# Entry of the odd layer: ctx's sums behind the fourth tile, two query projections inside the chain, mask and sinks on ScalarE

## The chip, the cores and the metric

The kernel runs on one core of a Trainium2 chip. The metric is device microseconds of one launch; lower is better. TensorE (PE) multiplies matrices, VectorE (DVE), ScalarE (ACT) and GpSimd (POOL) do elementwise work, and SyncE (SP) issues transfers. The engines run on their own and meet at semaphores; each works its own queue in order.

## The reference

A transformer of two layers over 512 rows of x and 256 rows of a context (ctx), width 1024. Layer 0 (even) mixes with a gated MLP and differential attention, layer 1 (odd) with banded attention over x's keys plus all keys of ctx; each layer is followed by a gated FFN. What matters here is the odd layer's entry:

```
a  = rmsnorm(h,  norm1_g) * (1 + sc1)  + sh1        # 512 rows
ac = rmsnorm(hc, norm1_g) * (1 + csc1) + csh1       # 256 rows of ctx
q, k, v = split(a @ w_qkv)      # 1024, 256, 256 columns
kc, vc  = split(ac @ w_qkv[:, 1024:])
q, k = rope(q), rope(k)
# block of 128 queries: keys of 3 blocks (masked to |distance| <= 128) and all of ctx, plus a sink
p = softmax([q k^T / 8 + mask, q kc^T / 8, sink])
o = p[keys] @ v + p[ctx] @ vc
```

There are 16 query heads and 4 key heads of 64 columns.

## The kernel before

Rows lie along the free axis and columns of the model along the 128 partitions, eight tiles (k = 0 to 7) to the width of 1024. A product in near-fp32 precision is three matmuls (`mm3`, L110 to 117): high weights by high data, high by low, low by high. Weights arrive by DMA as fp32 ("raw"), ScalarE casts the high half and GpSimd subtracts to make the low half.

`seam` runs from the end of the FFN of layer 0 to the keys and values of layer 1. Most of its instructions go through `run`, which chains them: each stands on its engine behind the one written before. What isn't chained (rotations, stacks, copies) is placed by the scheduler of the framework, by written order as priority and by simulated times; `issue_after` puts an instruction behind a given one, and `high_priority` gives a block an earlier place in the written order.

The order in `seam`:
- last FFN products, residuals, and squares of h for the norm. `sums` multiplies the squares by a matrix of ones; `diagonal` makes the inverse root from the sums in nine small VectorE steps and a tenth that puts it on a diagonal ("q"); `spread` multiplies that by ones and so lays it over all partitions.
- x's norm gives rx. Then, by the string of steps at L1471, for each tile k: modulation of x ("t", and its low half "l"), residuals of ctx ("c"), weights ("w"), and the products named by `order` (L1455): "K3" is tile 3 of the keys, "V3" of the values, "s" ctx's sums, "d" ctx's spread. Before the change "s" stands behind K6 and sums two tiles, since GpSimd has added the squares of tiles 1 to 6 to tile 0.
- query projection 0 (`qps`, in the PSUM bank "fill"), then for each tile ctx's modulation and its products with the key and value weights (`k_c`, `v_c`).
- the rotation of the keys (`rope`: shuffle and a product on VectorE, a product and an add on GpSimd), their high and low stacks (`stack`), mask, identity and sinks, copies of the values.

`odd` rotates and stacks query projection 0, computes projections 1 to 7 (L1556; one bank "fill" for all but projection 1) and, per group g of four heads, attends: scores in a wide PSUM tile (L1584, L1592, mask L1589), maximum, exponential, transposes (L1621), products with the values (L1632). PSUM has eight banks: three "b", one "f", and either four singles or two wide tiles.

Of the kernel before, what the change touches and what calls it, by code (L numbers as in the profile page):

```python
# [27 lines left out]
class Builder:  # L28
# [235 lines left out]
        nc.gpsimd.tensor_tensor(sh, sh, tabs[1], ALU.mult)  # L264
        nc.gpsimd.tensor_tensor(out, out, sh, ALU.add)

    def stack_q(self, q, pool, T, tag, bufs, s=1.0, eng=None):
        nc = self.nc
        qa = pool.tile([P, T], F32R, name=self.uid("qa"), tag=tag, bufs=bufs)
        qb = pool.tile([P, T], F32R, name=self.uid("qb"), tag=tag, bufs=bufs)  # L270
        A, B = slice(0, 64), slice(64, 128)
        nc.scalar.mul(qa[A], q[A], s)
        nc.scalar.mul(qb[B], q[B], s)
        for lo, hi, X, Y in ((qa, qa, A, B), (qb, qb, B, A)):
            if s == 1.0:
                (eng or nc.vector).tensor_tensor(lo[Y], q[X], hi[X].bitcast(F32), ALU.subtract)
            else:
                nc.vector.scalar_tensor_tensor(lo[Y], q[X], s, hi[X].bitcast(F32), ALU.mult, ALU.subtract)
        return qa, qb
# [1032 lines left out]
    def seam(self, s2_part, Wl, ahead):  # L1312
# [32 lines left out]

        def square(who, m):
            T = (TX, TC)[who]
            sq[who, m] = Qp.tile([P, T], F32, name=self.uid("sq"), tag=f"sq{who}", bufs=8)
            run("ACT", nc.scalar.activation, sq[who, m], self.h(who, m), AF.Square)

        def add(key, who, to, m):
            run(key, {"DVE": nc.vector, "POOL": nc.gpsimd}[key].tensor_tensor, sq[who, to], sq[who, to], sq[who, m], ALU.add)

        def sums(ps, tiles, T):
            n = T // P
            for i, t in enumerate(tiles):
# [50 lines left out]
        sums(ps, [sq[0, m] for m in (0, 3, 7)], TX)  # L1407
        for m in (0, 1):
            c_residual(m)
        c_unit(2, self.bank)  # L1410
        for m in (3, 4):
            c_unit(m, self.single)
# [39 lines left out]
                run("PE", self.mm3, acc[4 + tb], [t[:, tb * P:(tb + 1) * P] for t in C[k]], v_w(k), k == tb == 0,  # L1452
                    k == KT - 1)

        order = iter("K0 V0 K1 V1 K2 V2 K3 V3 K4 V4 K5 V5 K6 s K7 V6 d V7".split())  # L1455
        csum = []

        def products(upto):
            for v in order:
                if v == "s":  # L1460
                    csum.append(self.single())
                    sums(csum[0], [sq[1, 0], sq[1, 7]], TC)
                elif v == "d":
# [6 lines left out]
        rests = {}  # L1470
# [21 lines left out]
        for k in range(KT):  # L1492
            t, c = Wq[k // 4], k % 4 * P
            run("PE", self.mm3, qps, (t[:, 0, c:c + P], t[:, 1, c:c + P]), X[k], k == 0, k == KT - 1)
        kc = self.single()
        kc = [kc[:, n * TC:(n + 1) * TC] for n in range(2)]
        b = self.bank()
# [8 lines left out]
        kfs = [Rt.tile([P, TA], F32, name=self.uid("kf"), tag="kf", bufs=2) for _ in range(2)]  # L1506
        K = []
        for n in range(2):
            self.rope(kps[n], kfs[n][:, :TX], tabs)
# [10 lines left out]

        for n in range(2):
            stack(n, slice(0, TX))
        for n in range(2):
            nc.scalar.copy(kfs[n][:, TX:], kc[n])
            stack(n, slice(TX, TA))
        mask = Rk.tile([P, 2, P], F32R, name="mask")
        identr = Rk.tile([P, P], F32R, name="identr")
        sink = Rk.tile([P, 16], F32, name="sink2")
        with tc.issue_after(self.tail["DVE"].ins):
            nc.vector.tensor_copy(mask, mraw.rearrange("p (a c) -> p a c", a=3)[:, 0::2, :])  # L1530
            nc.vector.tensor_copy(identr, self.ident)
            nc.vector.tensor_copy(sink, nsink)
            nc.vector.tensor_scalar(nsink, nsink, -1.0, None, ALU.mult)
        with tc.issue_after(self.tail["ACT"].ins):
            nc.scalar.activation(self.small(16), nsink, AF.Exp)
        V = []
        for tb in range(6):
            v = Rk.tile([P, TC], F32, name=f"v1_{tb}")
# [3 lines left out]
        self.close_ring()  # L1542
        self.ring, self.ring_cfg = kept
        Rt.release()
        self.kv = qps, X, Rk, tabs, K[0] + K[1], V, mask, identr, sink, nsink

    def odd(self):
        tc, nc, a = self.tc, self.nc, self.a
        self.wp.release()
        self.open_wide()  # L1550
        qps, X, Rk, tabs, K, V, mask, identr, sink, nsink = self.kv
        Rs = tc.alloc_tile_pool(name="att1", bufs=1, side="right", reuse_waits="tile")
        Qs = {}

        def project_q(n):
            ps = (self.bank if n == 1 else self.fill)() if n else qps  # L1556
            if n:
                with tc.issue_after(self.tail["ACT"].ins) if n < 3 else ExitStack():
                    W = self.blocks(a["q1"][n])
                self.dense(ps, W, X)  # L1560
            qf = Rs.tile([P, TX], F32, name=self.uid("qf"), tag="qf", bufs=2)
            self.rope(ps, qf, tabs)
            Qs[n] = self.stack_q(qf, Rs, TX, "sq", 16, 0.125)

        def softmax(g, i, rc):

# [39 lines left out]
        def part():  # L1606
            return Rs.tile([P, 512], F32, name=self.uid("pt"), tag="pt", bufs=6)
# [173 lines left out]
```

## Time and profile before

| | us |
|---|---|
| median of three runs | 1585.23 |
| lowest and highest | 1578.97, 1585.93 |
| profiled execution | 1583.56 |
| its span | 1581.5 |
| granted clock, mean over the span | 0.988 |

The span is what the profiler saw between the first and the last instruction; the execution's own time is 2.06 us more. The stage that is edited lies between about 905 and 1010 us of the span; attention runs until about 1190. In rows of the timeline the first number is the start and the second the length; matmuls are pipelined, so a matmul's cost is the distance to the next start. "x24" merges 24 records of one kind; a matmul on fp32 data that aren't split leaves two records. In brackets stands the idle time of the engine before the row, and who ended it.

### The profile page before, as it was taken

The numbers are of one execution on the slowest core, as the hardware profiler recorded it, in microseconds if no ns is written. First come the engines' busy times: TensorE is split into PE (matmuls) and PEld (weight loads), VectorE is DVE, ScalarE is ACT, GpSimd is POOL, SyncE is SP. The second block draws the span as 40 slices with busy tenths as digits, with TensorE's granted clock in tenths as the row PEclk, the third lists the DMA queues.
The fourth block names the chain that finished last, engine by engine and source line by source line (L and its number), as shares of the span: only waits on it lengthen the run. The fifth ranks groups of instructions, "written<-read, shape, count | busy, mean of one in ns | idle before, by whom it ended". The sixth has DMA issues, their size and how long they took to land.

```text
span 1581.5 us, 24959 instructions
## 1 busy us (share of the span) xinstructions
PE 1520.5 (96%) x9547; PEld 1355.7 (86%) x9547; DVE 1082.6 (68%) x1942; ACT 728.7 (46%) x1486; POOL 831.6 (53%) x562
## 2 busy tenths in 40 slices
PE   6999988999999999999999998999999999999998
PEld 4776877889989999999999987777869989999997
DVE  4720788765697787888786478665667976666665
ACT  2412676553553333333333345555655644444444
POOL 0463211060356776777776454531304399898982
PEclk9999999999999999999999999999999999999999
DMA  9845100033123333444552211100225233333301
GB/s 329 309 143 190 40 8 1 1 133 134 67 75 119 114 110 118 140 160 141 166 167 67 74 58 42 61 28 4 72 81 198 68 96 106 97 107 105 100 21 54
DMA packets 53415, 162.26 MB, mean 103 GB/s; under 512 B 6192, under 2 KB 8624, under 8 KB 45616
## 3 DMA queue, kind: packets, MB, share of 16 engines
q1 hardware_dynamic: 46240, 135.37, 25.6%
q10 hardware_dynamic: 7056, 25.30, 4.9%
q8 instruction: 75, 1.23, 0.3%
q14 instruction: 44, 0.36, 0.1%
HBM read 158.55 MB, written 2.10 MB: 102 GB/s over the span
## 4 chain that ended last, share of the span: by engine, by line
PE 85%; DVE 10%; ACT 3%; issue 1%; POOL 0%; DMA 0%; DVEq 0%; SPq 0%; ACTq 0%; POOLq 0%
PE pw L114 11%; PE pw L115 11%; PE pw L116 11%; PE pb L115 9%; PE pb L114 8%; PE pb L116 8%; PE pf L114 4%; PE pf L115 4%; PE pf L116 4%; PE pb L1632 2%; PE pb L1621 2%; PE pf L370 2%; PE pw L1584 1%; PE pw L1592 1%; PE pw L553 1%
## 5 line engine op out<-in xcount | busy, mean ns | idle before, releaser
L114 PE MATMUL pw<-ax,w 128*128 128x384 f32 (+2 forms) x732 | 233.9, 321 | 2.5 <-DVE q L49 1.9
L115 PE MATMUL pw<-ax,w 128*128 128x384 f32 (+2 forms) x732 | 233.8, 320 | 1.4 <-DVE ax L477 1.4
L116 PE MATMUL pw<-ax,w 128*128 128x384 f32 (+2 forms) x732 | 233.2, 319 | 0.1
L785 DVE SCALAR_TENSOR_TENSOR xT<-pb,mod,xT 128x512 f32<-128x512 f32 (+3 forms) x206 | 144.1, 706 | 128.8 <-PE pb L116 128.5
L91 POOL TENSOR_TENSOR w<-raw,w 128x512 fp32r<-128x512 f32 (+1 forms) x74 | 112.8, 1531 | 204.3 <-ACT w L88 182.0
L49 POOL TENSOR_TENSOR w<-raw,w 128x512 fp32r<-128x512 f32 x120 | 182.4, 1537 | 47.1 <-ACT w L49 47.0
L49 POOL TENSOR_TENSOR w<-t,w 128x512 fp32r<-128x512 f32 x99 | 148.1, 1499 | 56.0 <-ACT w L49 56.0
L114 PE MATMUL pb<-hh,w 128*128 128x512 f32 x480 | 171.4, 357 | 2.3 <-DVE xT L785 2.3
L116 PE MATMUL pb<-hh,w 128*128 128x512 f32 x480 | 171.8, 358 | 0.3 <-DVE w L49 0.3
L115 PE MATMUL pb<-hh,w 128*128 128x512 f32 x480 | 171.5, 357 | 0.0
L115 PE MATMUL pw<-T,w 128*128 128x384 f32 (+1 forms) x508 | 157.0, 310 | 1.2 <-DVE T L131 1.2
L114 PE MATMUL pw<-T,w 128*128 128x384 f32 (+1 forms) x508 | 156.3, 310 | 1.1 <-DVE hs L49 1.1
L116 PE MATMUL pw<-T,w 128*128 128x384 f32 (+1 forms) x508 | 157.0, 310 | 0.0
L114 PEld LDWEIGHTS pw<-ax,w 128*128 128x128 f32 x732 | 139.0, 190 | 9.5 <-DVE q L49 2.6
L115 PEld LDWEIGHTS pw<-ax,w 128*128 128x128 f32 x732 | 139.3, 190 | 7.7 <-DVE ax L477 3.1
L116 PEld LDWEIGHTS pw<-ax,w 128*128 128x128 f32 x732 | 139.5, 191 | 3.0 <-DVE w L954 0.4
L114 PE MATMUL pf<-ax,w 128*128 128x256 f32 (+2 forms) x412 | 136.9, 332 | 3.9 <-ACT f L596 2.8
L115 PE MATMUL pf<-ax,w 128*128 128x256 f32 (+2 forms) x412 | 136.1, 330 | 0.8 <-POOL ax L131 0.8
L116 PE MATMUL pf<-ax,w 128*128 128x256 f32 (+2 forms) x412 | 135.6, 329 | 0.0
L49 POOL TENSOR_TENSOR hh<-hs,hh 128x768 fp32r<-128x768 f32 (+1 forms) x42 | 80.8, 1925 | 90.0 <-ACT hh L49 67.6
L49 POOL TENSOR_TENSOR w<-rawo,w 128x512 fp32r<-128x512 f32 x59 | 104.1, 1764 | 29.8 <-ACT w L49 29.8
L239 DVE SCALAR_TENSOR_TENSOR junk<-ar,cb 128x1024 bf16<-128x1024 f32 x64 | 105.7, 1652 | 0.0
(403 smaller groups left out, 3961.4 us busy)
## 6 DMA issues: line engine op xcount, KB each, us to landing
raw<-ffn_in SPq DMA_DIRECT2D x44, 1024.0 KB, 5.2
ar<-ada SPq DMA_DIRECT2D x24, 1024.0 KB, 7.2
ar<-ada ACTq DMA_DIRECT2D x48, 512.0 KB, 3.5
rawo<-ffn_out SPq DMA_DIRECT2D x88, 256.0 KB, 3.0
raw<-odd_out SPq DMA_DIRECT2D x32, 256.0 KB, 2.7
raw<-qk SPq DMA_DIRECT2D x16, 256.0 KB, 7.6
raw<-uv SPq DMA_DIRECT2D x16, 256.0 KB, 2.7
raw<-even_out SPq DMA_DIRECT2D x8, 512.0 KB, 3.5
```

The source lines that it names most:

```text
L49: self.tail[key] = fn(*args, **kw)
L91: eng.tensor_tensor(lo, raw, hi.bitcast(F32), ALU.subtract)
L114: mm(out, s[0], m[0], start=start, stop=False, **kw)
L115: mm(out, s[0], m[1], start=False, stop=False, **kw)
L116: return mm(out, s[1], m[0], start=False, stop=stop, **kw)
L239: return self.nc.vector.scalar_tensor_tensor(junk, t, 1.0, self.cb[who], ALU.mult, ALU.mult, accum_out=self.acc[who][:, col:col + 1])
L370: nc.tensor.matmul(ps[32 * q:32 * q + 32, :w], cst[:, k, :], t[:, w * q:w * q + w], start=k == 0, stop=k == KT - 1, skip_group_check=True)
L553: nc.tensor.matmul(ps[:, :TX], Q[c][:, qs], K[c][p][:, :TX], start=p == 0, stop=p == 1)
L785: ins = self.nc.vector.scalar_tensor_tensor(h, ps[:, r], self.modcol(l, j, m, who), h, ALU.mult, ALU.add)
L1584: nc.tensor.matmul(ps[:, st:en], Q, K[g][p][:, b0 * P:b1 * P], start=p == 0, stop=p == 1, skip_group_check=True)
L1621: last = nc.tensor.transpose(pt[:, x * P:(x + 1) * P], es[2 * (x % 2) + x // 2][:, kb * P:(kb + 1) * P], self.ident)
L1632: nc.tensor.matmul(po[64 * h:64 * h + 64, :], V[vb][:, 64 * g:64 * g + 64], t[:, h * TC:h * TC + TC], start=kb == 0, stop=kb == nb - 1, sk ...
```

## The change

Four things in `seam`, two in `odd`:
- `order` has "s" behind V4 and sums six tiles; VectorE adds the square of tile 1 to tile 0, GpSimd that of tile 2. K7 stands behind V6. Squares of x that are only added to others share two buffers.
- the weights of query projection 1 are loaded and split in the chain as well (at "l7"), and the projection itself follows projection 0, in a single bank.
- mask, identity, sinks, their negation and the first exponential are chained on ScalarE behind the weights, where they stood on VectorE behind ctx's modulation.
- the keys' rotation is written before the query projections; each half of the keys is stacked for x and ctx before the other half.
- `odd` rotates and stacks queries 0 and 1 at the priority of the place behind the first half of the keys, into tiles in the pool of the keys; the wide PSUM pool opens behind them.
- the loop over groups projects queries from 2 on.

```diff
-    def stack_q(self, q, pool, T, tag, bufs, s=1.0, eng=None):
+    def stack_q(self, q, pool, T, tag, bufs, s=1.0, eng=None, out=None):
-        qa = pool.tile([P, T], F32R, name=self.uid("qa"), tag=tag, bufs=bufs)
-        qb = pool.tile([P, T], F32R, name=self.uid("qb"), tag=tag, bufs=bufs)
+        qa, qb = out or [pool.tile([P, T], F32R, name=self.uid(v), tag=tag, bufs=bufs) for v in ("qa", "qb")]
...
-            sq[who, m] = Qp.tile([P, T], F32, name=self.uid("sq"), tag=f"sq{who}", bufs=8)
+            tag, n = ("sqc", 8) if who else ("sqx", 3) if m in (0, 3, 7) else ("sqt", 2)
+            sq[who, m] = Qp.tile([P, T], F32, name=self.uid("sq"), tag=tag, bufs=n)
...
         for m in (0, 1):
             c_residual(m)
+        add("DVE", 1, 0, 1)
...
-        order = iter("K0 V0 K1 V1 K2 V2 K3 V3 K4 V4 K5 V5 K6 s K7 V6 d V7".split())
+        order = iter("K0 V0 K1 V1 K2 V2 K3 V3 K4 V4 s K5 V5 K6 V6 K7 d V7".split())
...
-                    sums(csum[0], [sq[1, 0], sq[1, 7]], TC)
+                    sums(csum[0], [sq[1, m] for m in (0, 3, 4, 5, 6, 7)], TC)
...
-                products(f"V{k}" if k < 5 else "V5" if k == 5 else "s" if k == 6 else "K7")
-            if v == "l4":
-                for m in range(1, 7):
-                    add("POOL", 1, 0, m)
-            elif v == "l5":
+                products(f"V{k}" if k < 7 else "K7")
+            if v == "l1":
+                add("POOL", 1, 0, 2)
+            elif v in ("l5", "l7"):
                 wide, (self.ring, self.ring_cfg) = (self.ring, self.ring_cfg), kept
-                Wq = [part(*load(a["q1"][0][:, c:c + 512])) for c in (0, 512)]
+                Wq.append([part(*load(a["q1"][len(Wq)][:, c:c + 512])) for c in (0, 512)])
                 self.ring, self.ring_cfg = wide
         csum.append(diagonal(csum[0], TC))
         products("V7")
-        qps = self.fill()
...
+        run("ACT", nc.scalar.copy, mask, mraw.rearrange("p (a c) -> p a c", a=3)[:, 0::2, :])
+        run("ACT", nc.scalar.copy, identr, self.ident)
+        run("ACT", nc.scalar.copy, sink, nsink)
+        run("ACT", nc.scalar.mul, nsink, nsink, -1.0)
+        run("ACT", nc.scalar.activation, self.small(16), nsink, AF.Exp)
+        kfs = [Rt.tile([P, TA], F32, name=self.uid("kf"), tag="kf", bufs=2) for _ in range(2)]
+        for n in range(2):
+            self.rope(kps[n], kfs[n][:, :TX], tabs)
+        qps = [self.fill(), self.single()]
+        for ps, W2 in zip(qps, Wq):
+            for k in range(KT):
+                t, c = W2[k // 4], k % 4 * P
+                run("PE", self.mm3, ps, (t[:, 0, c:c + P], t[:, 1, c:c + P]), X[k], k == 0, k == KT - 1)
...
         for n in range(2):
             stack(n, slice(0, TX))
-        for n in range(2):
             nc.scalar.copy(kfs[n][:, TX:], kc[n])
             stack(n, slice(TX, TA))
...
+            if n == 0:
+                here = tc.cur_priority
...
+        stacks = [Rk.tile([P, TX], F32R, name=self.uid(t), tag="sq01", bufs=4) for _ in range(2) for t in ("qa", "qb")]
 
         def project_q(n):
-            ps = (self.bank if n == 1 else self.fill)() if n else qps
-            if n:
+            ps = self.fill() if n > 1 else qps[n]
+            if n > 1:
...
-            qf = Rs.tile([P, TX], F32, name=self.uid("qf"), tag="qf", bufs=2)
+            qf = Rs.tile([P, TX], F32, name=self.uid("qf"), tag="qf", bufs=2) if n > 1 else self.tmp()
             self.rope(ps, qf, tabs)
-            Qs[n] = self.stack_q(qf, Rs, TX, "sq", 16, 0.125)
+            Qs[n] = self.stack_q(qf, Rs, TX, "sq", 12, 0.125, out=stacks[2 * n:2 * n + 2])
...
+        with tc.high_priority(offset=tc.cur_priority - self.here):
+            for n in range(2):
+                project_q(n)
+        self.wp.release()
+        self.open_wide()
         for g in range(4):
-            project_q(2 * g)
-            project_q(2 * g + 1)
+            if g:
+                project_q(2 * g)
+                project_q(2 * g + 1)
             attend(g, 0)
```

More of the change, by code (lines that the diff above doesn't have):

```diff
@@ L1468, in products @@
                     return
-        rests = {}
+        rests, Wq = {}, []
         for v in "t0 c5 l0 w t1 c6 t2 l1 w c3 t3 l2 w c4 t4 l3 w c7 t5 l4 t6 l5 t7 l6 l7".split():
@@ L1490, in seam @@
         products("V7")
-        qps = self.fill()
-        for k in range(KT):
-            t, c = Wq[k // 4], k % 4 * P
-            run("PE", self.mm3, qps, (t[:, 0, c:c + P], t[:, 1, c:c + P]), X[k], k == 0, k == KT - 1)
+        mask = Rk.tile([P, 2, P], F32R, name="mask")
+        identr = Rk.tile([P, P], F32R, name="identr")
+        sink = Rk.tile([P, 16], F32, name="sink2")
+        run("ACT", nc.scalar.copy, mask, mraw.rearrange("p (a c) -> p a c", a=3)[:, 0::2, :])
[11 more added lines that the diff above has]
+                run("PE", self.mm3, ps, (t[:, 0, c:c + P], t[:, 1, c:c + P]), X[k], k == 0, k == KT - 1)
         kc = self.single()
@@ L1505, in seam @@
                 v_c(k - 1)
-        kfs = [Rt.tile([P, TA], F32, name=self.uid("kf"), tag="kf", bufs=2) for _ in range(2)]
         K = []
-        for n in range(2):
-            self.rope(kps[n], kfs[n][:, :TX], tabs)
         for n in range(2):
@@ L1522, in seam @@
             stack(n, slice(0, TX))
-        for n in range(2):
             nc.scalar.copy(kfs[n][:, TX:], kc[n])
             stack(n, slice(TX, TA))
[L1526 to L1535, printed above, removed]
+            if n == 0:
+                here = tc.cur_priority
         V = []
@@ L1544, in seam @@
         Rt.release()
+        self.here = here
         self.kv = qps, X, Rk, tabs, K[0] + K[1], V, mask, identr, sink, nsink
@@ L1548, in odd @@
         tc, nc, a = self.tc, self.nc, self.a
-        self.wp.release()
-        self.open_wide()
         qps, X, Rk, tabs, K, V, mask, identr, sink, nsink = self.kv
```

## The prediction

> **What bounds the kernel now.** I began with the page: who is busy, and what the chain that ended last consists of.
>
> ```profile
> span 1581.5 us, 24959 instructions
> PE 1520.5 (96%) x9547; PEld 1355.7 (86%) x9547; DVE 1082.6 (68%) x1942; ACT 728.7 (46%) x1486; POOL 831.6 (53%) x562
> PE 85%; DVE 10%; ACT 3%; issue 1%; POOL 0%; DMA 0%; DVEq 0%; SPq 0%; ACTq 0%; POOLq 0%
> raw<-q SPq DMA_DIRECT2D x16, 256.0 KB, 2.7
> ```
>
> TensorE is busy 96% of the span and is 85% of the chain: a change pays only by removing TensorE's waits, or its stretches at a lower clock. So I asked next who made TensorE wait from 905 to 1010 us, the stage that is edited (from, by whom, total, times, longest), and then the same stage cut into 5 us stretches (after the engines: granted clock, DMA share, GB/s).
>
> ```profile
> PE pw L49 <- DVE q L49: 4.8, 1, 4.8
> PE pw L1584 <- DVE qa L278: 1.8, 1, 1.8
> PE pf L114 <- DVE qf L263: 1.0, 2, 0.8
> ```
>
> ```profile
> 950.00:955.00 5.00, 1.58 (x13) 1.38 (x11) 4.93 (x9) 0.73 (x2) 4.56 (x4) 0.91 0.00 0
> 955.00:960.00 5.00, 3.65 (x15) 3.47 (x16) 4.79 (x11) 4.00 (x8) 0.43 (x1) 0.50 0.00 0
> 990.00:995.00 5.00, 4.17 (x13) 3.35 (x14) 4.83 (x7) 0.97 (x3) 4.84 (x4) 0.67 0.35 92
> ```
>
> Two waits matter, and behind each the granted clock falls: to 0.50 over 955 to 960 us and to 0.67 over 990 to 995. The timeline of TensorE gives the places (start, length of the record; the next row's start ends the work).
>
> ```profile
> 943.52 0.40 PE L114 MATMUL pw<-ax,w 128*128 128x512 f32 x1
> 947.73 1.05 PE L49 MATMUL pw<-ones,sq 128*128 128x128 f32 x8
> 948.53 0.48 PE L114 MATMUL pw<-ax,w 128*128 128x512 f32 x1
> 956.36 1.22 PE L49 MATMUL pw<-q,ones 128*128 128x256 f32 x2 [4.77 <-DVE q L49]
> 957.01 0.78 PE L114 MATMUL pb<-w,ax 128*128 128x256 f32 x1
> 959.93 0.63 PE L114 MATMUL pf<-ax,w 128*128 128x512 f32 x1
> 965.88 0.28 PE L114 MATMUL pw<-ax,w 128*128 128x256 f32 x1
> 977.39 0.40 PE L114 MATMUL pb<-ax,w 128*128 128x512 f32 x1
> 982.86 0.39 PE L114 MATMUL pf<-ax,w 128*128 128x512 f32 x1
> ```
>
> From the top: K5, V5 and K6 (943.52), ctx's sums ("s"), K7 and V6, which end at 956.36 - 4.77 = 951.59, a wait of 4.77 us, the spread "d", V7, query projection 0 (959.93), ctx's keys and values (965.88), query projection 1 (977.39), projection 2 (982.86). VectorE says why "d" was late:
>
> ```profile
> 948.81 0.16 DVE L49 TENSOR_SCALAR sm<-pw 128x2 f32<-128x2 f32 x1 [5.09 <-PE pw L49]
> 949.61 0.74 DVE L262 STREAM_SHUFFLE sh<-pw 128x512 f32<-128x512 f32 x1
> 954.26 1.19 DVE L49 SCALAR_TENSOR_TENSOR sm<-sm,sm 128x2 f32<-128x2 f32 x1
> 955.88 0.42 DVE L49 SCALAR_TENSOR_TENSOR q<-sm,ident 128x256 f32<-128x256 f32 x1
> ```
>
> It sat idle for 5.09 us, from 943.7, until the sums came, and then the ten small steps of the inverse root (948.81 to 956.3) were interleaved with the rotation of the keys (949.61), whose GpSimd half slowed the steps to 1.19 us each, against 0.16 for the first. The same ten steps for x's rows, with nothing in between, are the yardstick:
>
> ```profile
> 920.50 2.84 PE L49 MATMUL pf<-ones,sq 128*128 128x128 f32 x24
> 923.10 0.36 PE L114 MATMUL pb<-hh,raw 128*128 128x256 f32 x1
> 923.38 0.16 DVE L49 TENSOR_SCALAR sm<-pf 128x4 f32<-128x4 f32 x1 [1.97 <-PE pf L49]
> 925.15 0.69 DVE L49 SCALAR_TENSOR_TENSOR q<-sm,ident 128x512 f32<-128x512 f32 x1
> ```
>
> **The change part by part.** *Sums behind the fourth tile.* "s" now follows V4, at 943.52, and not K6, at 947.73. It sums six squares, 24 records, and no longer two, 8 records. Price on the path: 8 records took 948.53 - 947.73 = 0.80 us; 24 took 923.10 - 920.50 = 2.60 us; **+1.80 us**. The sums end near 946.2, the ten steps need 925.15 + 0.69 - 923.38 = 2.46 us, so "q" is there near 949. Now K5, V5, K6, V6, K7 lie in front of "d", which TensorE reaches at 951.59 + 1.80 = 953.4. Four microseconds are over, and the keys' rotation can't slip in, since it waits for K7, which ends then. **The wait of 4.77 us goes.**
>
> GpSimd's six adds become one on VectorE (a 256-column add, put into the 1.97 us of idle time in front of 923.38) and one on GpSimd, which has time between two weight halves; both at nothing on that cover. Squares m = 1, 2, 4, 5, 6 of x share two buffers; GpSimd had added the first two well before ScalarE wants them again, so nothing.
>
> *Clock behind that wait.* Projection 0 took 965.88 - 959.93 = 5.95 us for 24 matmuls, projection 1, the same work, 982.86 - 977.39 = 5.47, or 0.228 each. V7 took 959.93 - 957.01 = 2.92 us; K5, V5 and K6 took 4.21, the two K being six matmuls each at 0.228, which leaves 1.47 for V5, the same work as V7. So 1.45 + 0.48 = **-1.93 us**.
>
> *Second query projection in the chain.* It moves 5.47 us of TensorE from behind ctx's keys to in front; the sum stays. Its weights: two more transfers of 256 KB in a ring of three raw buffers, so the fourth waits until GpSimd has read the first.
>
> ```profile
> 939.32 5.00 POOL L49 TENSOR_TENSOR sq<-sq,sq 128x256 f32<-128x256 f32 x5
> 944.27 2.54 POOL L49 TENSOR_TENSOR w<-raw,w 128x512 fp32r<-128x512 f32 x2
> 954.24 0.62 ACT L1516 CAST kh<-kf 64x512 fp32r<-64x512 f32 x1 [12.10 <-POOL kf L265]
> ```
>
> Without the five adds the first half is read by about 942; issue to landing is 2.7 us on the page, so the fourth lands near 945.5. ScalarE's queue stands at that cast from about 943, and mask, sinks and the exponential (with its table load) are behind it. Nothing else is there: in front of the keys' casts at 954.24 it was idle for 12.10 us. TensorE wants these weights at 961. At nothing. The four small steps that leave VectorE stood behind ctx's modulation and in front of ctx's part of the key stacks, which the casts ended last (the row at 977.84, below): at nothing.
>
> *What it moves for ctx.* "d" at 953.4, V7 to 955.3, projections 0 and 1 to 966.3: ctx's modulation on VectorE gets 12 us before TensorE asks for it, where it had 8.9. Keys and values of ctx end near 977.8.
>
> *The entry of attention.* Rows there:
>
> ```profile
> 976.87 0.65 ACT L1524 COPY kf<-pw 128x256 f32<-128x256 f32 x2
> 977.84 1.88 DVE L1519 TENSOR_TENSOR kl<-kf,kh 64x256 fp32r<-64x256 f32 x4 [1.93 <-ACT kh L1516]
> 990.81 0.69 DVE L263 TENSOR_TENSOR qf<-pf,cos 128x512 f32<-128x512 f32 x1
> 990.83 0.38 PE L1584 MATMUL pw<-kh,qa 128*128 128x256 f32 x1 [1.76 <-DVE qa L278]
> 991.55 0.69 PE L114 MATMUL pf<-ax,w 128*128 128x512 f32 x1
> 995.30 0.39 PE L114 MATMUL pf<-ax,w 128*128 128x512 f32 x1
> 1000.47 0.50 PE L114 MATMUL pf<-ax,w 128*128 128x512 f32 x1 [0.76 <-DVE qf L263]
> ```
>
> The wait of 1.76 us was for the stack of query 1. That is now projected 11 us before the first score can run, so its stack is no longer last. Nine matmuls from 991.55 to 995.30 took 3.75 us, at 0.228 each 2.05: the slow stretch is 1.70. Together **-3.46 us**.
>
> What is late next? First, ctx's columns of the keys: copied, cast and subtracted, they were ready 1.9 us after ctx's products (976.87 to about 978.8). TensorE's cover is projection 2, whose weights were cast before. Second, projection 3 must wait until projection 2 is rotated out of the one "fill" bank (the row at 990.81 ended as 991.55 began). I bound the new wait by 0 (scores and transposes cover it) and by 3.46 (a wait as long as the old one, clock included), and take **+0.8**, the like wait of 0.76 at 1000.47, behind which the first matmul took 0.50 us, and not the 0.69 of 991.55.
>
> Here a rule bears on the clock. In the trace a wait of 1.76 us is followed by 0.67 in the slice from 990 us, and I count the slow 1.70 us to the wait. The Trainium skill, TensorE: Matmul & The Clock Gate, Part 1, has the clock halved only after an idle window of about 3.4 us. By that rule the slow stretch isn't the wait's, its 1.70 us would stay, and the time below would be 1577.7; the trace disagrees with the rule, as no wait that long stands there.
>
> **Sum.** -4.77 - 1.93 + 1.80 - 3.46 + 0.8 = -7.6 us. The profiled execution took 1583.56 us (2.1 above its span), 1.7 under the median of 1585.23 and inside its runs. So **1576 us**. With TensorE busy for 96% of the span, the shift should be kept to the end. From no change I can tell apart about 0.5%, 8 us; the forecast stands at that edge: -0.5% against the profiled execution, -0.6% against the median.
>
> **The rivals.**
>
> *The entry stalls.* If the written order has a score with ctx's columns, or projection 3, at the head of TensorE's queue before it is ready, the 3.46 comes back in full in place of 0.8: 1583.6 - 7.6 + 2.7 = **1578.7**. For: exactly this happened at 989. Against: projection 2 is ready as cover.
>
> *The wait at "d" stays.* If VectorE gets to the ten steps late or rotation is put in front again, only the price of the sums and the second wait remain: -3.46 + 0.8 + 1.80 = -0.9, **1582.7**. Against: VectorE is idle from 943.7 in that stretch.
>
> *VectorE is crowded under ctx's products.* From 954 it has two key rotations (2.8 us), sixteen modulation steps at 0.48 (7.7), eight key subtractions at 0.69 (5.5), two copies, and newly two query rotations (2.8) and two subtractions: 21 us, to be done by the last tile of ctx near 976. One microsecond over, at quiet prices.
>
> ```profile
> L49 DVE SCALAR_TENSOR_TENSOR t<-ctxT,mod,pw 128x256 f32<-128x256 f32 x8 | 3.8, 480 | 0.2
> 958.53 2.78 DVE L1519 TENSOR_TENSOR kl<-kf,kh 64x512 fp32r<-64x512 f32 x4
> L278 DVE SCALAR_TENSOR_TENSOR qb<-qf,qb 64x512 fp32r<-64x512 f32 x3 | 3.9, 1309 | 0.1
> ```
>
> A query's subtraction, made while GpSimd worked, took 1.31 us on the mean. Ten of them at 1.31 add 6 us, TensorE waits about 5 and loses some 2 of clock: 1576 + 7 = **1583**. It decides from 1 us of slowing on. Against: planned order gives modulation the lead, and TensorE trailed it by over a microsecond before. The Trainium skill, GPSIMD Engine Reference, section on the shared interfaces, says that VectorE's instructions with two SBUF inputs contend with GpSimd; the row agrees.
>
> *Handovers of the one bank, slower than before.* Projections 2 to 7 hand on "fill" five times, each behind a rotation on a crowded VectorE. They cost 1.0 us over two waits now. Were four of the five as long as the wait at 989, clock included, that is 13.8 against the 0.8 counted: 1576 + 13 = **1589**. It decides from three such handovers on. For: the order of the whole attention is planned anew from a start 5 us earlier. Against: with scores between them, only two waited before.
>
> **How the numbers follow.** Forecast 0.50 (own range 1572 to 1578), entry stalls 0.20, "d" stays 0.06, crowded 0.12, handovers 0.12. The range from 1571 to 1587 leaves out most of the handovers and gains beyond the waits seen. At the 0.5% edge a little of the forecast falls to "same", and of the handovers most count as slower: faster 0.48, same 0.39, slower 0.13.
>
> **What would show it.** Right: no wait of TensorE at the spread, clock 1.00 from 945 to 977, 24 records of sums at 943.5, "q" done by 950, projections 0 and 1 back to back, first scores near 980. Wrong: a wait at a matmul of ctx's keys (crowded), at L1584 or L1592 (entry), repeated waits of "pf" on "qf" (handovers), or ScalarE still at the fourth cast when the keys' casts are due.

## The result, and the profile after

The changed kernel took 1577.47 us (median of six runs, 1574.68 to 1577.93) beside 1585.38 us of the kernel before (six runs): a ratio of 0.9956, 95% interval 0.9944 to 0.9968. The profiled execution took 1574.68 us with a span of 1572.8, against 1583.56 and 1581.5; the mean clock went from 0.988 to 0.990. The forecast was 1576.

From the page of the changed kernel, span, engines and chain: TensorE's busy share rose to 97%, its busy time hardly moved.

```profile
span 1572.8 us, 24991 instructions
PE 1517.9 (97%) x9563; PEld 1356.2 (86%) x9563; DVE 1075.2 (68%) x1939; ACT 728.5 (46%) x1490; POOL 827.9 (53%) x557
PE 85%; DVE 10%; ACT 3%; issue 1%; DMA 0%; DVEq 0%; SPq 0%; POOL 0%; ACTq 0%; POOLq 0%
```

TensorE's waits from 905 to 1010 us in the changed kernel (from, by whom, total, times, longest):

```profile
PE pw L115 <- DVE ax L49: 2.2, 1, 2.2
PE pw L1584 <- ACT e L1598: 1.8, 1, 1.8
PE pf L114 <- DVE qf L263: 1.1, 1, 1.1
```

The two waits of before (4.8 us at the spread, 1.8 us for query 1's stack) are gone, and two others stand in their place. TensorE's timeline of the changed kernel:

```profile
928.30 0.40 PE L114 MATMUL pw<-ax,w 128*128 128x512 f32 x1
942.67 2.84 PE L49 MATMUL pw<-ones,sq 128*128 128x128 f32 x24
945.27 0.47 PE L114 MATMUL pw<-ax,w 128*128 128x512 f32 x1
952.38 0.60 PE L49 MATMUL pw<-q,ones 128*128 128x256 f32 x2
954.24 0.40 PE L114 MATMUL pf<-ax,w 128*128 128x512 f32 x1
974.82 0.43 PE L115 MATMUL pw<-ax,w 128*128 128x256 f32 x1 [2.20 <-DVE ax L49]
975.04 0.41 PE L116 MATMUL pw<-ax,w 128*128 128x256 f32 x1
980.60 0.40 PE L114 MATMUL pf<-ax,w 128*128 128x512 f32 x1
989.19 0.39 PE L1584 MATMUL pw<-kh,qb 128*128 128x256 f32 x1 [1.77 <-ACT e L1598]
1007.14 0.50 PE L114 MATMUL pf<-ax,w 128*128 128x512 f32 x1 [1.10 <-DVE qf L263]
```

The spread (952.38) no longer waits. At ctx's sixth tile (974.82) stands the first new wait, and the matmuls behind it start 0.21 us apart where 0.12 is full pace. The same stage in slices (after the engines: granted clock, DMA share, GB/s):

```profile
950.00:955.00 5.00, 5.00 (x34) 4.55 (x33) 3.11 (x8) 0.90 (x3) 2.30 (x2) 1.00 0.00 0
955.00:960.00 5.00, 5.00 (x24) 4.13 (x23) 4.92 (x10) 4.10 (x8) 2.95 (x3) 1.00 0.00 0
970.00:975.00 5.00, 2.80 (x23) 2.60 (x23) 4.87 (x7) 0.60 (x2) 2.90 (x2) 1.00 0.00 0
975.00:980.00 5.00, 5.00 (x31) 5.00 (x31) 2.53 (x5) 3.11 (x6) 2.80 (x3) 0.66 0.03 7
990.00:995.00 5.00, 5.00 (x25) 4.14 (x24) 2.22 (x4) 3.22 (x7) 2.84 (x3) 1.00 0.24 81
```

The slow slice moved from 955 (0.50) and 990 (0.67) to 975 (0.66). VectorE's timeline shows both why the old wait went and where the new one comes from:

```profile
945.55 0.16 DVE L49 TENSOR_SCALAR sm<-pw 128x2 f32<-128x2 f32 x1 [2.09 <-PE pw L49]
947.38 0.42 DVE L49 SCALAR_TENSOR_TENSOR q<-sm,ident 128x256 f32<-128x256 f32 x1
951.89 0.73 DVE L262 STREAM_SHUFFLE sh<-pw 128x512 f32<-128x512 f32 x1
963.52 3.20 DVE L1528 TENSOR_TENSOR kl<-kf,kh 64x512 fp32r<-64x512 f32 x2
970.84 1.33 DVE L277 SCALAR_TENSOR_TENSOR qa<-q,qa 64x512 fp32r<-64x512 f32 x1
972.20 1.65 DVE L277 SCALAR_TENSOR_TENSOR qb<-q,qb 64x512 fp32r<-64x512 f32 x1
973.89 0.48 DVE L49 SCALAR_TENSOR_TENSOR t<-ctxT,mod,pw 128x256 f32<-128x256 f32 x1
```

The ten steps are done by 947.8, 4.6 us ahead of the spread, with nothing between them. But then a pair of key subtractions takes 3.20 us (quiet pairs take 1.39), and query 0's two subtractions stand ahead of the step "t" (973.89) for which TensorE waits. The second new wait, for the first exponentials at 989.19, comes by another way. ctx's last key product ends about 979.9, but ScalarE stands at a weight cast that waits 3.44 us for its transfer; only behind it does it copy ctx's keys, and VectorE is idle for 5.45 us:

```profile
981.60 0.62 ACT L88 CAST w<-raw 128x512 fp32r<-128x512 f32 x1 [3.44 <-DMA raw<-q]
982.13 0.64 ACT L1532 COPY kf<-pw 128x256 f32<-128x256 f32 x2
983.07 0.42 DVE L1539 COPY v<-pb 128x256 f32<-128x256 f32 x1 [5.45 <-ACT v L1539]
```

Where the 8.7 us of span came from, by the distance between starts on TensorE beyond full pace (0.228 us for 512 columns, 0.175 for 384, 0.12 for 256, 0.11 for 128), summed by stretch:

| stretch of the span, us | before | after | difference |
|---|---|---|---|
| the sums themselves | 0.80 | 2.60 | +1.8 |
| 950 to 970, excess | 7.29 | 0.16 | -7.1 |
| 970 to 980, excess | 0.01 | 3.94 | +3.9 |
| 980 to 1010, excess | 5.36 | 3.68 | -1.7 |
| 1010 to 1110, excess | 13.8 | 10.2 | -3.6 |

These come to -6.7; the stretches are cut at fixed times, so that work near an edge counts in one kernel and not in the other. x's first key product already starts 0.8 us earlier (928.30 against 929.07), ahead of the orders that were edited, where executions of one kernel differ by more (935.04 in another of the changed kernel). The remainder lies at the edges and behind 1110.

Since executions differ by some us in the 900 us ahead of it, I read one more length from each profile, the **stretch**: from x's first key product to the end of the fourth head group. The kernel before ends it with the first row, the changed one with the second: 1096.47 + 0.68 - 929.07 = 168.1 us, and 1088.65 + 0.68 - 928.30 = 161.0.

```profile
1096.47 0.68 DVE L1645 TENSOR_TENSOR o<-o,pb 128x512 f32<-128x512 f32 x1
```

```profile
1088.65 0.68 DVE L1645 TENSOR_TENSOR o<-o,pb 128x512 f32<-128x512 f32 x1
```

### The profile page after: what moved, and what is told of

Read it like the earlier page. It is cut to its first block, busy times and chain, and to the rows that moved or that the text cites. A ratio compares the mean times of both kernels' runs of the same rounds, so it can differ in the third digit from the quotient of the medians.

```text
span 1572.8 us, 24991 instructions
## 1 busy us (share of the span) xinstructions
PE 1517.9 (97%) x9563; PEld 1356.2 (86%) x9563; DVE 1075.2 (68%) x1939; ACT 728.5 (46%) x1490; POOL 827.9 (53%) x557
## 4 chain that ended last, share of the span: by engine, by line
PE 85%; DVE 10%; ACT 3%; issue 1%; DMA 0%; DVEq 0%; SPq 0%; POOL 0%; ACTq 0%; POOLq 0%
PE pw L114 11%; PE pw L115 11%; PE pw L116 11%; PE pb L115 8%; PE pb L114 8%; PE pb L116 8%; PE pf L114 4%; PE pf L115 4%; PE pf L116 4%; PE pb L1632 2%; PE pb L1621 2%; PE pf L369 2%; PE pw L1584 1%; PE pw L1592 1%; PE pw L552 1%
## 5 line engine op out<-in xcount | busy, mean ns | idle before, releaser
L115 PE MATMUL pw<-ax,w 128*128 128x384 f32 (+2 forms) x740 | 237.5, 321 | 3.6 <-DVE ax L49 2.2
L114 PE MATMUL pw<-ax,w 128*128 128x384 f32 (+2 forms) x740 | 237.5, 322 | 2.5 <-DVE q L49 1.9
L116 PE MATMUL pw<-ax,w 128*128 128x384 f32 (+2 forms) x740 | 237.0, 321 | 0.1
L49 POOL TENSOR_TENSOR w<-raw,w 128x512 fp32r<-128x512 f32 x122 | 185.6, 1537 | 48.8 <-ACT w L49 48.6
L115 PEld LDWEIGHTS pw<-ax,w 128*128 128x128 f32 x740 | 141.3, 191 | 10.4 <-DVE ax L476 3.1
L114 PEld LDWEIGHTS pw<-ax,w 128*128 128x128 f32 x740 | 141.1, 191 | 9.7 <-DVE q L49 2.7
L116 PEld LDWEIGHTS pw<-ax,w 128*128 128x128 f32 x740 | 141.5, 191 | 3.4 <-DVE w L953 0.4
```

The costliest lines, as they stand in the source:

```text
L49: self.tail[key] = fn(*args, **kw)
L114: mm(out, s[0], m[0], start=start, stop=False, **kw)
L115: mm(out, s[0], m[1], start=False, stop=False, **kw)
L116: return mm(out, s[1], m[0], start=False, stop=stop, **kw)
```

## The experiments

My theory after the result: the sums' move frees the spread, query 1 frees the entry, and VectorE ahead of ctx's products takes part of it back. The rivals: one part carries it all; or attention's order does.

**One part at a time.** First the kernel before with the sums alone moved.

```diff
-K4 V4 K5 V5 K6 s K7 V6 d V7
+K4 V4 s K5 V5 K6 V6 K7 d V7
...
-sums(csum[0], [sq[1, 0], sq[1, 7]], TC)
+sums(csum[0], [sq[1, m] for m in (0, 3, 4, 5, 6, 7)], TC)
...
```

> The kernel before with the sums of ctx alone moved (behind V4, six tiles, two adds), all else as before. Theory A (the change gains what it removes in front of the spread): the wait of 4.77 us and its slow stretch go, 1.8 us of sums are added, so 4.9 us less than before, and no wait of TensorE at the spread; the wait of 1.8 us for the stack of query 1 stays. Theory B (the gain comes mostly from the attention being ordered anew once query 1 is in the chain): the wait at the spread turns up again one step later, and the time is within 2 us of before.

Measured: 1583.87 us, ratio 1.0000 (0.9984 to 1.0016). Its profile is its longest execution (1590.18), and its stretch is 171.0 us: in neither measure is there a gain. The waits stand here (905 to 1020 us):

```profile
PE pf L114 <- DVE qf L263: 6.9, 4, 2.8
PE pw L115 <- DVE ax L49: 2.3, 2, 1.7
```

The wait of 4.8 us at the spread is gone, and TensorE waits 9.2 us for VectorE behind it: at ctx's products, and four times for a rotation to clear the one bank.

Then the changed kernel with the sums as they were, everything else of it kept:

```diff
-K4 V4 s K5 V5 K6 V6 K7 d V7
+K4 V4 K5 V5 K6 s K7 V6 d V7
...
```

> The changed kernel with the sums of ctx as before (behind K6, two tiles, five adds on GpSimd); query 1 in the chain and mask and sinks on ScalarE stay. Theory A: the wait of about 4.8 us at the spread is back with its slow stretch, and only the entry of attention gains, 1 to 3 us less than before. Theory B: the attention stage, from projection 3 to its end, is shorter by some 4 us as in the changed kernel, and the time is 5 to 7 us under before.

Measured: 1577.44 us, ratio 0.9956 (0.9942 to 0.9969), the whole gain, although its profile has a wait of 5.44 us at the spread with 0.52 of clock behind it. There is no wait at ctx's products, and the stretch is 162.5 us. Then the four small steps on ScalarE alone:

```diff
-            nc.vector.tensor_copy(mask, mraw.rearrange("p (a c) -> p a c", a=3)[:, 0::2, :])
+        run("ACT", nc.scalar.copy, mask, mraw.rearrange("p (a c) -> p a c", a=3)[:, 0::2, :])
...
```

> The kernel before with mask, identity, sinks and the first exponential on ScalarE in the chain, all else as before. Theory A: these steps were on no path, within 1 us of before. Theory B (VectorE's work in front of ctx's part of the key stacks is on the path): up to 4 us less, with the scores of attention starting earlier.

Measured: 1584.56 us, ratio 1.0006 (0.9993 to 1.0020), stretch 168.2: nothing, as priced. So what pays is query 1 in the chain with the early stacks; the sums' move pays nothing that the totals can measure, with it or without (the stretch is 162.5 us without the move and 161.0 with it, each from one or two profiles). No run parts query 1's stack from query 0's. The kernel before made both behind ctx's products (the first and the last of the four subtractions):

```profile
985.03 1.10 DVE L278 SCALAR_TENSOR_TENSOR qa<-qf,qa 64x512 fp32r<-64x512 f32 x1 [0.65 <-ACT qa L272]
992.13 1.57 DVE L278 SCALAR_TENSOR_TENSOR qb<-qf,qb 64x512 fp32r<-64x512 f32 x1
```

The changed kernel makes them from 970.84 to 977.1.

**Is it VectorE's place in the queue?** The changed kernel, with the VectorE work of queries 0 and 1 (rotation and stack) behind ctx's modulation.

```diff
             for n in range(2):
-                project_q(n)
+                with tc.issue_after(self.tail["DVE"].ins):
+                    project_q(n)
```

> The changed kernel with VectorE's part of the rotation and stacks of queries 0 and 1 put behind ctx's modulation. Theory C (the wait of 2.2 us at ctx's sixth tile, with 1.6 us of slow clock, is VectorE doing query work ahead of the modulation): both go, and the time is 3 to 4 us under the changed kernel, about 0.9933 of before. Theory D (the query work only moves the wait): the stacks are late for the first scores, TensorE waits 2 us or more there, and the time equals that of the changed kernel, 0.9956, or is over it.

Measured: 1581.47 us, ratio 0.9988 (0.9973 to 1.0004), stretch 166.3. With the projection in the chain but the stacks late, most of the gain is lost. The wait at ctx's products went, and the entry took more than it gave:

```profile
985.57 0.39 PE L1584 MATMUL pw<-kh,qa 128*128 128x256 f32 x1 [1.84 <-DVE qa L277]
988.63 0.80 PE L114 MATMUL pf<-ax,w 128*128 128x512 f32 x1 [2.21 <-DVE qf L263]
```

Next, the changed kernel with other work moved out of the way: the low halves of the second keys (groups 2 and 3) behind ctx's modulation.

```diff
-                for Z in (X, Y):
-                    nc.vector.tensor_tensor(kl[Z, c], k, kh[X, c].bitcast(F32), ALU.subtract)
+                with tc.issue_after(after.ins) if after else ExitStack():
+                    for Z in (X, Y):
+                        nc.vector.tensor_tensor(kl[Z, c], k, kh[X, c].bitcast(F32), ALU.subtract)
...
```

> The changed kernel with one thing moved: VectorE's eight low halves (L1528) of the second keys' stacks over x's columns (keys of groups 2 and 3, which attention first reads some 50 us later) are put behind ctx's modulation. Nothing is left out. Theory (VectorE's queue is what ctx's products wait for: between 955 and 975 us it is busy 4.9 of every 5 us, and two of these pairs, 3.20 and 1.39 us, stand ahead of ctx's sixth tile): the wait of 2.20 us at 974.82 and the slow clock behind it go, 3.9 us less, about 1573.5 us, ratio 0.993, if the entry to attention stays at its 1.77 and 1.10 us of waits. Rival A (the late pairs, 2.8 us, come ahead of query 1's stack on VectorE and the first scores wait for it): the wait moves to the entry, about 1577, ratio 0.9955. Rival B (TensorE's wait ends with ScalarE or GpSimd, not VectorE): the wait of 2.2 us stays, 1577.

Measured: 1577.11 us, ratio 0.9969 (0.9958 to 0.9980), stretch 161.5. Rival A: no wait at ctx's products, but 3.27 us at the entry for the first exponentials, and 1.14 for a low half of ctx's keys. The late subtractions, four and not the eight of the expectation, took 5.88 us beside GpSimd's weight halves (2.8 quiet), ahead of query 1's stack:

```profile
975.08 5.88 DVE L1529 TENSOR_TENSOR kl<-kf,kh 64x512 fp32r<-64x512 f32 x4
980.99 0.69 DVE L277 SCALAR_TENSOR_TENSOR qa<-q,qa 64x512 fp32r<-64x512 f32 x1
```

The same edit on the kernel with the sums alone:

> The kernel before with ctx's sums behind the fourth tile (as in the run with the sums alone, ratio 1.0) and with the second keys' low halves over x's columns behind ctx's modulation. Nothing is left out. Theory (the sums' own gain, 6.7 less 1.8 us, was taken back by VectorE's queue ahead of ctx's products, 1.66 and 0.63 us with slow clock, in that run): the products wait no more and about 2 to 4 us of it appear, 1580 to 1582, ratio 0.9975 to 0.9985. Rival (it was taken back by the entry: rotations and stacks of queries 0 and 1 late on VectorE, four waits of the one bank for rotations, 6.9 us): nothing appears, since the late halves crowd the entry more: 1584 to 1588, ratio 1.0 to 1.002.

Measured: 1580.64 us, ratio 0.9989 (0.9980 to 0.9998), stretch 166.2. A gain of 0.1%: the waits at ctx's products went, and one of 3.78 us for query 0's rotation came, which stands behind ctx's key stacks on VectorE. Without the early stacks of the queries, little of the sums' gain got through in these two runs.

**Is it the order of attention?** In the changed kernel projection 7 runs behind the first head group, in the kernel before ahead of its end. So the kernel before with only that:

```diff
-                self.dense(ps, W, X)
+                self.dense(ps, W, X, after=self.first if n == 7 else None)
...
```

> The kernel before with one thing moved: the products of the eighth query projection (number 7) are held behind the last transposes of the first head group (L1643), as the order of the changed kernel has it. Nothing is left out. Theory (the place of this projection is what the attention of the changed kernel gains by: excess over full pace between 1010 and 1110 us 8.1 against 12.2): attention is 3 to 4 us shorter, 1580.5 us, ratio 0.9975. Rival (the gain in attention comes from the earlier scores of the first group, ahead of the third projection, and projection 7 only follows from it): no change or a loss, since the first group's last block loses its filler work: 1584 to 1587, ratio 1.0 to 1.002.

Measured: 1583.95 us, ratio 1.0009 (0.9997 to 1.0021), stretch 168.4. The place of projection 7 is worth nothing by itself. Nor does it go along with earlier first scores: in the run with the queries behind, the first score starts 53.8 us behind x's first key product, in the changed kernel 57.1, and yet that run has projection 7 where the kernel before has it.

**Three waits, one queue?** If the spread, ctx's products and the entry are separate prices, they can be taken away one by one. The changed kernel with the four query subtractions alone behind ctx's modulation, the rotations left in place:

```diff
-                nc.vector.scalar_tensor_tensor(lo[Y], q[X], s, hi[X].bitcast(F32), ALU.mult, ALU.subtract)
+                with self.tc.issue_after(after.ins) if after else ExitStack():
+                    nc.vector.scalar_tensor_tensor(lo[Y], q[X], s, hi[X].bitcast(F32), ALU.mult, ALU.subtract)
...
```

> The changed kernel with one thing moved: VectorE's four subtractions that end the stacks of queries 0 and 1 (L277) are put behind ctx's modulation; the rotations stay where they are. Nothing is left out. Theory (the 1.33 and 1.65 us of query 0's two subtractions, at 970.84 and 972.20, are the last thing ahead of ctx's sixth tile on VectorE): without them the tile is modulated 3.0 us earlier, the wait of 2.20 us at 974.82 and its slow clock go (3.9 us), and the first scores, which read the stacks from 985.4 on, don't wait, since query 1's subtractions end at 977.1 as before or up to 1.4 us later: 1573.5 to 1574.5, ratio 0.993. Rival (what is taken from ctx's products comes back at the entry, as it did in the run with the late keys and in the run with both queries' VectorE work behind the modulation): 1576 to 1578, ratio 0.9950 to 0.9965.

Measured: 1577.63 us, ratio 0.9967 (0.9954 to 0.9980), stretch 162.2. The rival: the 2.2 us at ctx's products are gone and 5.11 us stand at the entry.

The chain alone, with the keys' rotation held behind the ten steps of ctx's scale:

```diff
-        for n in range(2):
-            self.rope(kps[n], kfs[n][:, :TX], tabs)
+        with tc.issue_after(self.tail["DVE"].ins):
+            for n in range(2):
+                self.rope(kps[n], kfs[n][:, :TX], tabs)
...
```

> The run with the chain alone (ctx's sums where the kernel before has them), and the keys' rotation put behind the ten small steps of ctx's scale. Nothing is left out. Theory of the wait at the spread (the steps are ready in time and are stretched by the rotation's multiplies between them and by GpSimd's beside them): the wait of 5.44 us and its slow clock, 7.5 us of excess, go without moving the sums at all, and without their 1.8 us; VectorE's crowd ahead of ctx's products then costs up to the 3.9 us that it costs in the changed kernel: 1573.5 to 1577.5, ratio 0.9935 to 0.9955. Rival (the steps are late because the sums are late): a wait of 2 us or more stays at the spread: 1576 to 1578, ratio 0.995 to 0.9965.

Measured: 1575.01 us, ratio 0.9958 (0.9945 to 0.9972), stretch 161.2. From 940 to 1012 us:

```profile
PE pw L1585 <- ACT e L1599: 3.5, 1, 3.5
PE pw L115 <- DVE ax L49: 1.6, 1, 1.6
PE pf L114 <- DVE qf L263: 1.1, 1, 1.1
PE pw L49 <- DVE q L49: 0.5, 1, 0.5
```

The wait at the spread fell from 5.44 to 0.54 us with the sums left where they were: it was the rotation among the steps, not the lateness of the sums. But waits of 1.6 and 3.5 us now stand at ctx's products and at the entry, and the stretch is that of the changed kernel, 161.2 against 161.0. Both edits together:

> Both of the two others: the chain alone, the keys' rotation behind ctx's scale, and the stacks' subtractions of queries 0 and 1 behind ctx's modulation. Nothing is left out. Theory (the wait at the spread, the wait at ctx's products and the sums' 1.8 us are three separate prices, and none comes back): 1571.5 to 1573, ratio 0.992. Rival (the products wait behind the keys' low halves as much as behind the subtractions, or the entry takes it back): 1575 to 1578, ratio 0.9945 to 0.9965.

Measured: 1574.00 us, ratio 0.9948 (0.9929 to 0.9967), stretch 160.6. No wait at ctx's products, 0.47 at the spread, 4.85 at the entry. The changed kernel again, on the same chip:

> The changed kernel itself, beside the three others on the same chip, to compare them with. Both theories: 1577, ratio 0.9955, with the wait of 2.2 us at ctx's sixth key product.

Measured: 1577.06 us, ratio 0.9961 (0.9948 to 0.9974), stretch 160.9, with 2.17 us at ctx's sixth tile and 3.08 at the entry. Its profile is an execution 8 us longer than the first one's, and the stretch is the same, so the stretch does leave out what lies ahead. The median of the run with both behind is 3 us lower, but the intervals overlap and the stretches differ by 0.3 us, so I don't call it better.

**Taking the work away.** The rotation and the subtractions behind, and four of VectorE's subtractions left out: this kernel does not compute the low halves of the second keys over x's columns.

```diff
-                    nc.vector.tensor_tensor(kl[Z, c], k, kh[X, c].bitcast(F32), ALU.subtract)
+                    if n and c.start == 0:
+                        with tc.issue_after(self.tail["ACT"].ins):
+                            nc.scalar.copy(kl[Z, c], k)
...
```

> The run with the rotation and the subtractions behind, and four of VectorE's subtractions left out, so its output is not the reference's: the low halves of the second keys' stacks over x's columns are not computed, ScalarE writes a copy of the keys in their place behind ctx's modulation (four of 0.62 us in a gap of 2.7 us). It measures what VectorE's queue is worth and is no version to use. Theory (VectorE, 38.0 of 40 us busy from 951 to 991 us, is what sets the first scores' way to the first exponentials, so that a wait taken away ahead of ctx's products comes back at the entry): without these four (2.65 and 1.39 us) the first row maxima come 3 to 4 us earlier, the wait of 4.85 us at the entry falls to 1 to 2 us, and the stretch from x's first key product to the end of the fourth head group falls from 160.6 to 157 to 158 us; about 1571, ratio 0.9925 to 0.9935. Rival (the entry hangs on another chain, ctx's key products and ScalarE's copies of them): the entry's wait stays at 4 us or more, the stretch at 160 us or more, 1574 to 1577.

Measured: 1568.58 us (1568.27 to 1568.68), ratio 0.9912 (0.9896 to 0.9928), stretch 155.7. The window from 951 to 991 us (PE, PEld, DVE, ACT, POOL busy, clock, DMA share, GB/s), first of the run that does this work, then of the one that leaves it out:

```profile
951.00:991.00 40.00, 34.68 (x214) 31.11 (x212) 38.04 (x67) 21.86 (x44) 22.09 (x17) 0.98 0.15 50
```

```profile
951.00:991.00 40.00, 38.05 (x227) 33.62 (x226) 33.12 (x62) 25.79 (x53) 22.74 (x17) 1.00 0.14 46
```

With VectorE busy 38.0 of 40 us, TensorE worked 34.7; with VectorE at 33.1, TensorE worked 38.1. Where the work is left out, the entry's wait is 1.43 us:

```profile
984.33 0.39 PE L1590 MATMUL pw<-kh,qb 128*128 128x256 f32 x1 [1.43 <-ACT e L1604]
```

The four subtractions had cost 2.65 + 1.39 us; the stretch fell by 4.9, more than I expected: 3.4 us by the wait, the rest by the clock, which was 0.50 from 989.1 to 992.5 behind the longer wait and 1.00 here. So in the run with both behind, VectorE's queue, from the keys' rotation to the first row maxima, is what this stage lasts. A version that does the four in a quiet place later, behind the first maxima, wasn't tried.

The changed kernel itself isn't so full: VectorE works 32.6 us in this window, and the chain to its first exponentials starts at the weight cast on ScalarE (981.60). In its second execution ScalarE stands at the same cast until 988.15, about 3 us after ctx's last key product. No clock was lost at ctx's products there (1.00 where the first execution had 0.50), yet the entry wait is 1.3 us longer and the stretch the same. So what is saved in front can come back at ScalarE's queue as well as at VectorE's. This rival, the weight transfer at the entry, wasn't tested; a run with that cast behind the copies of ctx's keys would do it, and by the rows at most the wait of 1.77 us (an estimate) is to be had directly.

| run | stretch, us | ratio |
|---|---|---|
| before | 168.1 | 1 |
| sums alone | 171.0 | 1.0000 |
| scalar steps alone; projection 7 late | 168.2; 168.4 | 1.0006; 1.0009 |
| queries behind; sums and late keys | 166.3; 166.2 | 0.9988; 0.9989 |
| chain alone | 162.5 | 0.9956 |
| changed; subtractions behind; late keys | 161.0; 162.2; 161.5 | 0.9956; 0.9967; 0.9969 |
| rotation behind; both behind | 161.2; 160.6 | 0.9958; 0.9948 |
| four subtractions left out | 155.7 | 0.9912 |

Among the complete kernels with the queries stacked early the stretches lie within 2 us of each other, whether the wait stands at the spread, at ctx's products or at the entry.

## Why the prediction was right, and where not

The total was right, 1576 against 1577.5, and that in part by luck: a loss of 3.9 us at ctx's products and a gain of 3.6 us in attention, neither of them in the sum, nearly cancel. Two terms were right in place and size. One of the forecast's own signs of being wrong, a wait at a matmul of ctx's keys, appeared.

*Sums.* +1.80 predicted; 24 records from 942.67 to 945.27 are 2.60 us against 0.80. Right. The ten steps were due near 949 and were done by 947.8.

*The wait at the spread and the clock behind it.* -6.7 predicted, -7.1 measured at the place. Right, but the reason given was only half of it: the rotation behind the steps alone brings the wait to 0.54 us, without moving the sums. (Of the ten steps before, two took 1.19 us, not each; the rotation's own instructions on VectorE took about 2.5 us between them.)

*ScalarE and the fourth weight half, at nothing.* The cast waited 2.47 us for its transfer, until 943.97, and the small steps behind it were over by 947; the run with them alone is at 1.0006. Right.

*ctx's modulation.* Here a step failed. I gave it "12 us before TensorE asks for it, where it had 8.9", and put the crowded VectorE among the rivals at 0.12, since "planned order gives modulation the lead". It didn't: a key pair of 3.20 us and two query subtractions of 1.33 and 1.65 stood ahead of "t". The mechanism of that rival happened, at 3.9 us and not 7. Its list of work also had two query subtractions where there are four, 1.4 us too little at quiet prices.

*The entry.* -2.7 predicted (-3.46 and +0.8), -1.7 measured. The wait for query 1's stack went; in its place came 1.77 us for the first exponentials and 1.10 for the bank: the +0.8 should have been about 1.8. The step that failed here is that ctx's key columns would be ready as soon after ctx's products as before (1.9 us). ScalarE began to copy them 2.2 us after the last key product, where it had begun 0.2 us after it, because the cast that waited for its weights stood in front. Handovers came once.

*Attention.* -3.6 us that I hadn't. In the runs it comes with early stacks of the queries: the six kernels with a stretch of 160.6 to 162.5 all have projection 7 behind the first head group and end the next three groups 23.1, 17.6 and 16.8 us apart, and those at 166 and over don't, the one with both queries' VectorE work behind among them. Projection 7's place alone doesn't bring it. Why the order comes with the stacks, and which of its many gaps of 0.2 to 0.8 us makes the gain, is open.

*The deeper fault* is that the terms were added as if each wait had its own cause. Here -6.7 + 1.8 for the sums is worth nothing that the totals can measure, because the time comes back 20 to 40 us later, at VectorE or at ScalarE; and query 1 with the early stacks is worth the whole gain by the totals, 5.6 us by the stretch, and not 2.7.

*The clock.* I counted 1.70 us of slow clock to a wait of 1.76, against the Trainium skill, TensorE: Matmul & The Clock Gate, Part 1, whose idle window is about 3.4 us. The changed kernel's wait of 2.20 us was followed by 0.66, shorter than that window again; but its 1.77 us was followed by 1.00. Neither the rule nor mine, that such a wait brings it, holds; the last section says what the slow stretches follow. The time by that rule, 1577.7, lies near the result, but what it rests on, a slow stretch that stays at the entry, didn't come (1.00 there).

## What to carry to other kernels

Add up the queue of the engine that releases the waits, from its first to its last release in the stage, at contended prices; if it fills the stage, a wait taken away in front comes back behind, and only work that leaves the queue (or its contention) counts. If it doesn't fill it, look for what it waits for in turn: here a copy on ScalarE that stood behind a weight cast, and the cast behind its transfer. Test it by leaving work out, which says in one run what it is worth. Read a stage's length between two fixed points of the profile, since the executions differ by more ahead of it than the edit moves.

## What the hardware showed that I had not expected

Whether the clock falls behind a wait isn't settled by its length alone. In two executions of the changed kernel the same wait stood at ctx's sixth tile: behind 2.20 us the granted clock was 0.54 for 3.7 us, behind 2.17 us it was 1.00; the second execution had 1.00 behind a wait of 3.08 us too, while the kernel before had 0.67 behind 1.76. These are the stretches right behind, first of the one execution, then two of the other:

```profile
974.80:978.50 3.70, 3.68 (x18) 3.69 (x19) 2.73 (x5) 3.31 (x7) 1.30 (x1) 0.54 0.00 0
```

```profile
981.00:986.00 5.00, 4.46 (x36) 4.46 (x37) 3.22 (x7) 3.72 (x7) 2.07 (x2) 1.00 0.00 0
995.00:1000.00 5.00, 4.27 (x22) 3.68 (x23) 2.34 (x6) 2.99 (x8) 3.66 (x3) 1.00 0.34 105
```

What the traces show in its place is a grid. In each of the fourteen profiles all stretches at 0.50 begin at multiples of 3.413 us from one another and last one or two such windows, but for the last of a profile. In the kernel before two begin at 954.15 and 991.69, eleven windows apart; in the second execution of the changed kernel the nearest begin at 471.93 and 1178.49, 207 windows apart, and 980.51 is 149 windows behind the first of them. Cut by its grid, the same wait lies in one window of the first execution and is shared by two of the second (the number behind the length is TensorE's busy time):

```profile
971.61:975.02 3.41, 1.21 (x10) 1.01 (x9) 3.31 (x5) 0.62 (x2) 1.62 (x2) 1.00 0.00 0
975.02:978.43 3.41, 3.41 (x17) 3.41 (x17) 2.51 (x5) 3.09 (x6) 1.23 (x1) 0.50 0.00 0
```

```profile
977.10:980.51 3.41, 2.27 (x19) 2.06 (x18) 3.35 (x3) 0.00 (x0) 2.85 (x2) 1.00 0.00 0
980.51:983.92 3.41, 2.38 (x20) 2.38 (x21) 3.25 (x8) 2.75 (x6) 0.00 (x0) 1.00 0.00 0
```

The first leaves TensorE idle for 2.20 us of one window, and the next window is at 0.50; the second leaves it idle for 1.14 and 1.03, and the clock stays at 1.00. So it is with the others: the wait of 1.76 us of the kernel before lies whole in one window (988.28 to 991.69), and the one of 3.08 us is cut into 1.50 and 1.57. From 900 to 1107 us of all fourteen profiles, every window at full clock with 1.76 us or more of idle TensorE was followed by one at 0.50 (15 of them), and none with 1.70 or less was, which is about half the window. Elsewhere in the span that border is less sharp, between about 1.5 and 1.9 us, and what decides there I can't say. So a kernel that waits for 2 to 3 us pays for the clock in some executions and not in others, by where the wait falls on the grid.

And a 64x512 subtraction on VectorE took 0.69 us with GpSimd quiet, and 1.65 to 1.68 beside GpSimd's adds (972.20 in the changed kernel) and weight halves (in the run with both behind).
